# Where the low parts of split weights and of the indexer's doubled keys and queries are subtracted: from GpSimd to VectorE, in the projections of a two-layer hybrid decoder

## The chip, the cores and the metric

The kernel runs on one NeuronCore of one Trainium2 chip. The metric is the device time of one execution, in microseconds (us); lower is better. The engines are named as the profile names them: PE (TensorE; PEld is its weight load), DVE (VectorE), ACT (ScalarE), POOL (GpSimd) and SP (the queue that issues most transfers). Each engine takes its instructions strictly in the order of its own queue.

## The reference, cut to what matters

Two layers work on 1024 prompt tokens and 32 sample tokens (8 sequences of 4). In each layer a normalised activation `h` goes through one combined input projection, whose columns feed four groups of heads; then come attention and recurrences, an output projection, and a gated feed-forward block.

```python
h = rmsnorm(x, lp["norm1_g"]) * (1.0 + sc1) + sh1
p = split_cols(h @ lp["w_in"])
...
sc = jnp.einsum("bqhd,bsd->bqhs", iq, ik).astype(jnp.float32) * IDX_DIM ** -0.5
score = jnp.einsum("bqh,bqhs->bqs", iw.astype(jnp.float32) * IDX_HEADS ** -0.5, jax.nn.relu(sc))
score = jnp.where(k_pos[None, :] <= q_pos[:, None], score, -jnp.inf)
val, idx = lax.top_k(score, topk)
```

The last four lines are the indexer: 8 small heads give each query a score for each key, and the 256 best keys are kept.

## The kernel before, in words

A product of float32 matrices is made from three products of rounded parts: each operand is split into a high part (the value in the matmul's fp32r format) and a low part (value less high part), and high x high, high x low and low x high are summed in PSUM (`dense_c`, line 478, and `dense_n`, line 498). For weights the split is done by `unit` (line 453): a block of 1024 x 256 weights arrives in two halves of 128 x 1024 elements in `wr`; for each half ACT casts it to `wh` (line 461), and POOL subtracts `wh` from `wr` and writes `wl` (line 462). Two blocks of `wh` and `wl` exist at a time, so the cast for a block waits until PE has finished the block two before it.

In a layer the stages follow each other: input projection with the indexer and the top-k selection, attention and recurrences, output projection, feed-forward block. The input projection has twelve such blocks: `idx_q` in `first_units`, then `lru_x` and `lru_gate` (`t_unit`), seven blocks by `nat_unit`, and `gla_q`/`gla_k` and `gla_g` (`t_unit`). After each tile of a projection `background` advances side work: the indexer (`idx_prompt`), its top-k (`topk_prompt`), the samples' index and selection, and the RG-LRU. The output projection and the feed-forward block call `unit` too; at the start of each layer a small block of 128 columns (`misc_aps`) is split as well.

The indexer's keys and queries are doubled in place by `dup` (line 737): each 32-wide vector is laid out as high and low part, ACT casting (line 743) and POOL subtracting (line 744), into tiles of 128 x 512 (`ikd`, `iqd`). The attention code calls the same `dup` for its own tiles (`dup`, 128 x 1024).

The top-k of the prompt runs on DVE and ACT: for each of 31 bits a round compares six rows of scores with a threshold and counts (line 833 on DVE for four of the rows, tiles `tkb` and `tku`; line 830 on ACT for the other two, tile `tks`), and then updates the threshold by a few instructions on 128 x 6 elements (lines 852 to 858, 879 to 885 on DVE). Then six rows are finished with a scan (line 903). The samples' selection does the like with 128 x 1 elements (lines 1001 to 1063). The rotary embedding of a projected tile is two multiplications on DVE and POOL (lines 526, 528, 529) and an addition on DVE (line 530).

The order on each engine is made by a scheduler, which plays the program through a timeline of its own when the kernel is built, and emits the instructions as they come up there. Any change of an instruction's engine therefore moves many others.

```python
def unit(wp, rp, aps, width, n=2, first=None):
    ...
        with soon(HP2):
            act.copy(hi[:, ks, :width], raw[:, :, :width])
            pool.tensor_tensor(lo[:, ks, :width], raw[:, :, :width], hi[:, ks, :width].bitcast(F32), op=sub)
```

Of the kernel before, what the change touches and what calls it, by code (L numbers as in the profile page):

```python
# [10 lines left out]
F32 = mybir.dt.float32  # L11
# [129 lines left out]
def trunk(ctx, tc, io, out, dbg=None, depth=DEPTH, stop=99):  # L141
    nc = tc.nc
    dve, act, pool, pe, sp = nc.vector, nc.scalar, nc.gpsimd, nc.tensor, nc.sync
    mult, add, sub = OP.mult, OP.add, OP.subtract
# [56 lines left out]
    def soon(n):  # L201
        return tc.high_priority(n) if n else nullcontext()
# [230 lines left out]
    def raw_piece(rp, aps, width, i, n, nr):  # L433

        kk = 8 // n
        raw = rp.tile([128, kk, 256], F32, tag="wr", name="wr", bufs=nr)
        if sum(a.shape[1] for _, a in aps) < width:
            pool.memset(raw[:, :, :width], 0.0)
        for c0, a in aps:
            sp.dma_start(raw[:, :, c0:c0 + a.shape[1]],  # L440
                         a[kk * 128 * i:kk * 128 * (i + 1), :].rearrange("(k p) m -> p k m", p=128))
        return raw
# [4 lines left out]
    def weights(name):  # L447

        rp = tc.tile_pool(reuse_waits="tile", name="wr" + name, bufs=2)
        wp = tc.tile_pool(reuse_waits="tile", name="w" + name, bufs=2)  # L450
        return rp, rp.__enter__(), wp, wp.__enter__()

    def unit(wp, rp, aps, width, n=2, first=None):

        hi = wp.tile([128, 8, 256], F32R, tag="wh", name="wh", bufs=2)
        lo = wp.tile([128, 8, 256], F32R, tag="wl", name="wl", bufs=2)
        for i in range(n):
            raw = first[i] if first else raw_piece(rp, aps, width, i, n, 2)
            ks = slice(8 // n * i, 8 // n * (i + 1))
            with soon(HP2):  # L460
                act.copy(hi[:, ks, :width], raw[:, :, :width])  # L461
                pool.tensor_tensor(lo[:, ks, :width], raw[:, :, :width], hi[:, ks, :width].bitcast(F32), op=sub)  # L462
        return hi, lo

    def split2(parts_, c, g, raw):
# [173 lines left out]
    wrpool, wrp, wpool, wp_ = weights("0")  # L639
    mw = unit(wp_, wrp, misc_aps(0), 128)  # L640
    for l in range(depth):
# [25 lines left out]
        def background():  # L667
            advance(side, TK)
            advance(tops, TT)
            if count[0] % ADH == 0:  # L670
                advance(late)
            count[0] += 1
            if count[0] % SELH == 0:
                advance(sel)

        def col(name, c0=0, n=256):
            return w_in[:, OFF[name] + c0:OFF[name] + c0 + n]

        def nat_unit(name):
            w = unit(wp_, wrp, [(0, col(name))], 256)  # L680
            for i in range(9):
                nat_tile(name, w, i)
                background()
# [14 lines left out]
                sp.dma_start(st[name][t0:t0 + n, :], nat[:n, :])  # L698

        def t_unit(specs, aps, width):  # L700
            w = unit(wp_, wrp, aps, width)
            for j, (key, n) in enumerate(specs):
                def done(c, cs, p):
                    with soon(HP1):
                        e = hp.tile([128, CWM], F32, tag="nat", name="te", bufs=3)[:, :CHK[c][1]]
                        act.copy(e, p)
                        sp.dma_start(stt[key][:n, cs], e[:n, :])
                    background()
                dense_t(w, j, h, done, HPD)

        def first_units():

            rope_t.append(const("rope", where=hp).rearrange("p (i w) -> p i w", i=9))
            w = unit(wp_, wrp, [(0, col("idx_q"))], 256)
            mtp = tc.tile_pool(reuse_waits="tile", name="mt", bufs=1)
            mt = mtp.__enter__().tile([128, T], F32, name="mt")
            for c, (c0, cn) in enumerate(CHK):
                act.copy(mt[:, c0:c0 + cn], dense_c(mw, 0, h, c))
                for i in range(3 * c, 3 * c + 3):
                    nat_tile("idx_q", w, i)  # L720
                for i in range(3 * c, 3 * c + 3):
                    t0, n = TOK[i]
                    pm = bank("m")
                    pe.transpose(pm[:n, :128], mt[:, t0:t0 + n], ident)
                    nat = hp.tile([128, CWM], F32, name="nat", bufs=3)[:, :256]
                    raw = hp.tile([128, 256], F32, name="rraw", bufs=2)
                    act.copy(raw[:n, 0:32], pm[:n, 32:64])
                    act.copy(nat[:n, 32:40], pm[:n, 64:72])
                    tmp = hp.tile([128, 256], F32, name="rtm", bufs=2)
                    rope(nat[:n, 0:32], raw[:n, 0:32], i, n, 32, tmp[:n, 0:32], rope_t[0])  # L730
                    sp.dma_start(st["idx_k"][t0:t0 + n, :], nat[:n, 0:32])
                    sp.dma_start(st["idx_w"][t0:t0 + n, :], nat[:n, 32:40])
            sp.dma_start(stt["gla_a"], mt[0:16, :])
            mtp.__exit__(None, None, None)


        def dup(dst, src, nh, d, key):

            dv = dst.rearrange("p (n a b d) -> p n a b d", n=nh, a=2, b=2)
            s = src[:, :, None, :].to_broadcast([128, nh, 2, d])  # L740
            hi = dv[:, :, :, 0, :] if key else dv[:, :, 0, :, :]
            lo = dv[:, :, :, 1, :] if key else dv[:, :, 1, :, :]
            act.copy(hi, s)
            pool.tensor_tensor(lo, s, hi.bitcast(F32), op=sub)

        def stack_t(dst, srcs, idr=None):

# [10 lines left out]
        def idx_prompt():  # L758
            with tc.tile_pool(reuse_waits="tile", name="ix", bufs=2) as ix:
                kn = ix.tile([128, 8, 32], F32, name="ikn", bufs=1)  # L760
# [1 line left out]
                sp.dma_start(wix, st["idx_w"][0:TP, :].rearrange("(i p) d -> p i d", p=128))  # L762
                dve.tensor_scalar(wix, wix, 1.0 / 16.0, None, op0=mult)
                kd = ix.tile([128, 8 * 128], F32R, name="ikd", bufs=1)
                dup(kd, kn, 8, 32, True)
                kst = ix.tile([128, TP], F32R, name="ikst", bufs=1)
                yield
                stack_t(kst, [kd[:, i * 128:i * 128 + 128] for i in range(8)])
# [2 lines left out]
                def prep(i):  # L771
                    qn = ix.tile([128, 8, 32], F32, name="iqn")
                    sp.dma_start(qn, st["idx_q"][i * 128:i * 128 + 128, :].rearrange("p (h d) -> p h d", h=8))
                    qd = ix.tile([128, 8 * 128], F32R, name="iqd", bufs=1)
                    dup(qd, qn, 8, 32, False)
                    Q[i] = ix.tile([128, 8 * 128], F32R, name="iqst")
                    yield
                    stack_t(Q[i][:, :512], [qd[:, j * 128:j * 128 + 128] for j in range(4)])
                    yield
                    stack_t(Q[i][:, 512:], [qd[:, j * 128:j * 128 + 128] for j in range(4, 8)])  # L780
                yield from prep(2)
                for i in range(2, 8):
                    nxt = prep(i + 1) if i < 7 else iter(())
                    n = NB[i]
                    s = sc[:, so[i]:so[i] + n]
# [1261 lines left out]
        n = 0  # L2047
# [52 lines left out]
        wrpool, wrp, wpool, wp_ = weights(f"{l + 1}")  # L2100
# [54 lines left out]
        if True:  # L2155
# [58 lines left out]
            for q in range(11):  # L2214
# [67 lines left out]
                if q % 2 or q == 10:  # L2282
                    n = 4 if q % 2 else 2
# [8 lines left out]
                if pend is not None and q < 10:  # L2292
                    w = down_w(pend[0])
# [68 lines left out]
```

## Time and profile before

| | us |
|---|---|
| median of 3 runs | 3873.0 (3866.61 to 3873.54) |
| the profiled execution, its own time | 3873.57 |
| its span, first to last instruction | 3871.7 |
| mean granted TensorE clock | 0.948 of full speed |

| engine | busy us | share of the span |
|---|---|---|
| PE | 3522.8 | 91% |
| DVE | 2487.2 | 64% |
| ACT | 1502.2 | 39% |
| POOL | 1394.5 | 36% |

Busy is the time in which an engine has an instruction under way, including time in which that instruction is held up. The shares are means over stages with different limits; what bounds one stage is read from that stage alone.

### The profile page before, as it was taken

How to read it: one execution, taken by the hardware profiler on the slowest of the kernel's cores; microseconds unless marked ns; L12 is line 12 of the kernel's file. 1: busy time of each engine (PE TensorE's matmuls, PEld its weight loads, DVE VectorE, ACT ScalarE, POOL GpSimd, SP SyncE). 2: the span in 40 equal slices, each digit the busy share in tenths (PEclk: the TensorE clock that was granted, in tenths of full speed). 3: DMA queues.
4: the chain of work that ended last, by engine and by line, in shares of the span. 5: the costliest groups of instructions: out<-in, count | busy, mean ns of one | idle time of the engine just before them, and what ended most of it. 6: DMA issues, size and time to landing. Idle time of an engine off the chain costs nothing.

```text
span 3871.7 us, 64297 instructions
## 1 busy us (share of the span) xinstructions
PE 3522.8 (91%) x24916; PEld 3150.6 (81%) x24916; DVE 2487.2 (64%) x5662; ACT 1502.2 (39%) x3026; POOL 1394.5 (36%) x1241
## 2 busy tenths in 40 slices
PE   7999868899899999999989988588997999999998
PEld 4887765576689999999979877455766999999997
DVE  5479999677555444445564999985764655555555
ACT  4445554366533112211244547434764322112122
POOL 2344238524233222222334541564343223222231
PEclk7999888989999999999989999788999999999999
DMA  6452335536521332321123222455464011111111
GB/s 228 135 151 89 111 112 184 192 107 203 166 85 50 98 105 87 99 77 34 55 79 92 88 88 71 132 183 195 139 217 152 25 44 51 49 40 49 45 46 56
DMA packets 351404, 407.65 MB, mean 105 GB/s; under 512 B 93711, under 2 KB 299261, under 8 KB 349914
## 3 DMA queue, kind: packets, MB, share of 16 engines
q1 hardware_dynamic: 312186, 265.09, 22.6%
q0 software_dynamic: 38912, 138.43, 10.7%
q8 instruction: 197, 3.23, 0.3%
q14 instruction: 109, 0.89, 0.1%
HBM read 354.32 MB, written 58.04 MB: 107 GB/s over the span
## 4 chain that ended last, share of the span: by engine, by line
PE 65%; DVE 20%; issue 5%; DMA 4%; ACT 3%; POOL 2%; SPq 0%; another core or an unknown queue 0%; DVEq 0%; ACTq 0%; POOLq 0%
PE d L478 31%; PE m L2180 13%; DVE tkb L833 2%; PE d L1369 2%; DVE tku L833 2%; PE d L498 2%; PE e L1399 2%; PE e L1376 1%; PE m L1637 1%; PE d L330 1%; PE g L1796 1%; DVE ny L413 1%; PE m L1689 1%; DVE nat L526 1%; PE m L1696 1%
## 5 line engine op out<-in xcount | busy, mean ns | idle before, releaser
L478 PE MATMUL d<-h,wh 128*128 128x384 f32 (+1 forms) x5856 | 1406.8, 326 | 55.9 <-ACT h L468 18.0
L478 PEld LDWEIGHTS d<-h,wh 128*128 128x128 f32 x5856 | 1031.6, 190 | 72.0 <-ACT h L468 18.5
L478 PE MATMUL d<-h,wl 128*128 128x384 f32 (+1 forms) x2928 | 945.9, 326 | 7.5 <-POOL wl L462 7.5
L478 PEld LDWEIGHTS d<-h,wl 128*128 128x128 f32 x2928 | 557.2, 191 | 11.2 <-POOL wl L462 10.0
L462 POOL TENSOR_TENSOR wl<-wr,wh 128x1024 fp32r<-128x1024 f32 (+1 forms) x172 | 376.9, 2208 | 430.8 <-ACT wh L461 343.6
L498 PE MATMUL d<-wh,h 128*128 128x256 f32 (+1 forms) x2304 | 463.0, 296 | 46.8 <-ACT nat L697 28.5
L498 PEld LDWEIGHTS d<-wh,h 128*128 128x128 f32 (+1 forms) x2304 | 370.8, 191 | 65.7 <-ACT nat L697 32.7
L507 DVE SCALAR_TENSOR_TENSOR xT<-m,mod,xT 128x384 f32<-128x384 f32 (+1 forms) x480 | 273.2, 572 | 230.9 <-PE m L2180 230.4
L2180 PE MATMUL m<-mh,wdh 128*128 128x384 f32 (+1 forms) x1056 | 350.9, 332 | 0.4 <-DVE xT L507 0.4
L2279 POOL TENSOR_TENSOR ml<-z,mh 128x384 fp32r<-128x384 f32 x132 | 132.8, 1025 | 600.2 <-ACT mh L2278 600.2
L2180 PE MATMUL m<-ml,wdh 128*128 128x384 f32 (+1 forms) x1056 | 344.5, 326 | 0.0
L498 PE MATMUL d<-wl,h 128*128 128x256 f32 (+1 forms) x1152 | 338.4, 294 | 5.2 <-POOL wl L462 3.2
L2180 PE MATMUL m<-mh,wdl 128*128 128x384 f32 (+1 forms) x1056 | 342.5, 325 | 0.0
L461 ACT CAST wh<-wr 128x1024 fp32r<-128x1024 f32 (+1 forms) x172 | 158.1, 955 | 200.1 <-PE d L478 169.2
L498 PEld LDWEIGHTS d<-wl,h 128*128 128x128 f32 (+1 forms) x1152 | 220.2, 191 | 12.2 <-issue 6.2
L2250 DVE COPY fs<-G 128x2 f32<-128x2 f32 x44 | 50.8, 1156 | 278.2 <-ACT G L2230 278.2
L2230 ACT COPY G<-d 128x384 f32<-128x384 f32 x132 | 57.4, 442 | 420.3 <-PE d L478 392.4
L2180 PEld LDWEIGHTS m<-mh,wdh 128*128 128x128 f32 x1056 | 200.4, 190 | 9.1 <-issue 6.6
L2180 PEld LDWEIGHTS m<-ml,wdh 128*128 128x128 f32 x1056 | 200.6, 190 | 1.4 <-issue 0.9
L2180 PEld LDWEIGHTS m<-mh,wdl 128*128 128x128 f32 x1056 | 200.3, 190 | 0.0
L2170 POOL TENSOR_TENSOR wdl<-wr,wdh 128x1024 fp32r<-128x1024 f32 x44 | 104.9, 2416 | 264.0 <-ACT wdh L2169 264.0
L1369 PE MATMUL d<-c_ident,kv 128*128 128x128 f32 x1024 | 165.1, 295 | 16.3 <-ACT KT L210 7.5
(554 smaller groups left out, 6664.7 us busy)
## 6 DMA issues: line engine op xcount, KB each, us to landing
adaw<-in_w_ada_dram SPq DMA_DIRECT2D x80, 512.0 KB
wr<-in_w_in_dram SPq DMA_DIRECT2D x48, 512.0 KB
wr<-in_ffn_w_gate_dram SPq DMA_DIRECT2D x44, 512.0 KB
wr<-in_ffn_w_up_dram SPq DMA_DIRECT2D x44, 512.0 KB
wr<-in_ffn_w_down_dram SPq DMA_DIRECT2D x44, 512.0 KB
xd<-xT SPq DMA_DIRECT2D x16, 528.0 KB
adaw<-in_w_ada_dram SPq DMA_DIRECT2D x8, 1024.0 KB
wr<-in_w_out_dram SPq DMA_DIRECT2D x32, 256.0 KB
```

Of the source, the lines that this page charges most:

```text
L461: act.copy(hi[:, ks, :width], raw[:, :, :width])
L462: pool.tensor_tensor(lo[:, ks, :width], raw[:, :, :width], hi[:, ks, :width].bitcast(F32), op=sub)
L478: pe.matmul(pd, lhsT=w[a][:, k, j * 128:j * 128 + 128], rhs=h[b][c][:, k, :], start=(q == 0), stop=(q == 23))
L498: pe.matmul(pd[:n, :256], lhsT=h[b][c][:, k, t0:t0 + n], rhs=w[a][:, k, :], start=(q == 0), stop=(q == 23))
L507: dve.scalar_tensor_tensor(x[:, m, t0:t0 + n], p[:, :n], mod[:, gate + m, 0:1], x[:, m, t0:t0 + n], op0=mult, op1=add)
L833: dve.tensor_scalar(scratch[:, :n], src[:, s], thr[:, j:j + 1], None, op0=OP.is_ge, op1=add, accum_out=cnt[:, j:j + 1])
L1369: pe.transpose(pm[:, z_ * 128:z_ * 128 + 128], kg[:, j, f * 128:f * 128 + 128], ident)
L1399: pe.matmul(po[32 * j:32 * j + 32, :256], lhsT=wT[:, g, 32 * j:32 * j + 32], rhs=vg[:, j, :], start=(g == 0), stop=(g == 3))
L2170: pool.tensor_tensor(lo[:, z_, :], raw, hi[:, z_, :].bitcast(F32), op=sub)
L2180: pe.matmul(pd, lhsT=a, rhs=b, start=(n == 0), stop=(n == len(ops) - 1))
L2230: act.copy(Gp[:, 2 + CHK[c][0]:2 + CHK[c][0] + n], p[:, :n])
L2279: pool.tensor_tensor(ml[:, cs], z[:, cs], mh[:, cs].bitcast(F32), op=sub)
```

## The change

`unit` and `dup` get a parameter `eng`, by default POOL. The input projection's callers pass DVE: the twelve blocks of each layer (24 subtractions of 128 x 1024 elements a layer), and the indexer's seven tiles (128 x 512). The small block at a layer's start, the output projection, the feed-forward block and the attention's `dup` keep POOL. The arithmetic is the same.

```diff
-    def unit(wp, rp, aps, width, n=2, first=None):
+    def unit(wp, rp, aps, width, n=2, first=None, eng=pool):
...
                 act.copy(hi[:, ks, :width], raw[:, :, :width])
-                pool.tensor_tensor(lo[:, ks, :width], raw[:, :, :width], hi[:, ks, :width].bitcast(F32), op=sub)
+                eng.tensor_tensor(lo[:, ks, :width], raw[:, :, :width], hi[:, ks, :width].bitcast(F32), op=sub)
...
         def nat_unit(name):
-            w = unit(wp_, wrp, [(0, col(name))], 256)
+            w = unit(wp_, wrp, [(0, col(name))], 256, eng=dve)
...
         def t_unit(specs, aps, width):
-            w = unit(wp_, wrp, aps, width)
+            w = unit(wp_, wrp, aps, width, eng=dve)
...
         def first_units():
...
-            w = unit(wp_, wrp, [(0, col("idx_q"))], 256)
+            w = unit(wp_, wrp, [(0, col("idx_q"))], 256, eng=dve)
...
-        def dup(dst, src, nh, d, key):
+        def dup(dst, src, nh, d, key, eng=pool):
...
             act.copy(hi, s)
-            pool.tensor_tensor(lo, s, hi.bitcast(F32), op=sub)
+            eng.tensor_tensor(lo, s, hi.bitcast(F32), op=sub)
...
-                dup(kd, kn, 8, 32, True)
+                dup(kd, kn, 8, 32, True, dve)
...
-                    dup(qd, qn, 8, 32, False)
+                    dup(qd, qn, 8, 32, False, dve)
```

Two places show how the order moves. The first is on DVE, in the first layer's top-k, at the start of the 27th round of counting (`tku`: the compare-and-count of line 833; `tdf`, `tth`, `tcd`, `tnc`: the threshold's update; `wl`: the low part of the weights). Before:

```order
L884 TENSOR_TENSOR tdf<-cnt,tneed 128x6
L1040 TENSOR_SCALAR sdl<-spc 128x1
L885 SCALAR_TENSOR_TENSOR tth<-tdf,tth 128x6
L1041 SCALAR_TENSOR_TENSOR scand<-sdl,scand 128x1
L879 TENSOR_SCALAR tcd<-tth 128x6
L881 TENSOR_SCALAR tnc<-tth 128x6
L1037 TENSOR_SCALAR snc<-scand,scap 128x1
L833 TENSOR_SCALAR tku,cnt<-mk,tcd 128x384
L833 TENSOR_SCALAR tku,cnt<-mk,tcd 128x640
L833 TENSOR_SCALAR tku,cnt<-mk,tcd 128x768
```

With the change:

```order
L885 SCALAR_TENSOR_TENSOR tth<-tdf,tth 128x6
L879 TENSOR_SCALAR tcd<-tth 128x6
L881 TENSOR_SCALAR tnc<-tth 128x6
L1150 TENSOR_SCALAR lth_4995<-lth_4995,spt 128x1056
L833 TENSOR_SCALAR tku,cnt<-mk,tcd 128x384
L462 TENSOR_TENSOR wl<-wr,wh 128x1024
L833 TENSOR_SCALAR tku,cnt<-mk,tcd 128x640
L462 TENSOR_TENSOR wl<-wr,wh 128x1024
L1001 STREAM_TRANSPOSE srep<-scnt 128x32
L833 TENSOR_SCALAR tku,cnt<-mk,tcd 128x768
```

The two subtractions of the last block (`gla_g`) now stand inside the round, between its counts; before, they stood on POOL.

The second place is on ACT, at the casts that these two subtractions wait for (`tks`: ACT's counts, two a round; `nat`: the copy of a projected tile out of PSUM; `wh`: the cast). Before:

```order
L830 ACTIVATE tks,cnt<-mk,tnc 128x512
L1017 ACTIVATE selb,scnt<-ss,snc,sng 128x544
L697 COPY nat<-d 128x256
L830 ACTIVATE tks,cnt<-mk,tnc 128x896
L1146 ACTIVATE lth_4995<-m,hb 128x288
L697 COPY nat<-d 32x256
L461 CAST wh<-wr 128x1024
L1017 ACTIVATE selb,scnt<-ss,snc,sng 128x544
L461 CAST wh<-wr 128x1024
```

With the change:

```order
L1017 ACTIVATE selb,scnt<-ss,snc,sng 128x544
L830 ACTIVATE tks,cnt<-mk,tnc 128x512
L830 ACTIVATE tks,cnt<-mk,tnc 128x896
L1146 ACTIVATE lth_4995<-m,hb 128x288
L697 COPY nat<-d 32x256
L461 CAST wh<-wr 128x1024 x2
L1017 ACTIVATE selb,scnt<-ss,snc,sng 128x544
L830 ACTIVATE tks,cnt<-mk,tnc 128x512
```

Before, these casts stood behind 56 of ACT's counts, which is 28 rounds; with the change they stand behind 52, which is 26 rounds. The copy of the last `gla_v` tile stays just ahead of them.

## Rows read from the trace of the kernel before

**Rows 1.** The page's first line.

```profile
span 3871.7 us, 64297 instructions
```

**Rows 2.** Stretches: length, busy PE, PEld, DVE, ACT, POOL, clock, DMA share, GB/s.

```profile
130.00:195.00 65.00, 62.77 (x517) 56.38 (x515) 18.31 (x30) 27.63 (x56) 14.40 (x11) 0.97 0.54 159
390.00:455.00 65.00, 53.48 (x374) 49.52 (x372) 64.17 (x216) 40.34 (x78) 15.72 (x17) 0.89 0.35 110
2325.00:2390.00 65.00, 54.35 (x386) 50.35 (x386) 63.71 (x198) 46.01 (x89) 18.62 (x7) 0.97 0.29 90
```

**Rows 3.** Line 462, whole span: ns min/median/max, first and last start in us.

```profile
L462 POOL TENSOR_TENSOR wl<-wr,wh x172: 1261/2393/2984, 57.6 to 3759.2; 128x1024 fp32r<-128x1024 f32 x136, 128x512 fp32r<-128x512 f32 x36
```

**Rows 4.** Timeline of POOL: start, us, instruction, count.

```profile
299.07 4.72 POOL L462 TENSOR_TENSOR wl<-wr,wh 128x1024 fp32r<-128x1024 f32 x2
...
338.16 4.72 POOL L462 TENSOR_TENSOR wl<-wr,wh 128x1024 fp32r<-128x1024 f32 x2 [0.28 <-issue]
```

**Rows 5.** Timeline of DVE, first layer: a count and an update, then ten instructions.

```profile
301.61 1.28 DVE L833 TENSOR_SCALAR_CACHE_REDUCE tkb<-mk,cand 128x1024 bf16<-128x1024 bf16 x1
304.07 0.17 DVE L858 SCALAR_TENSOR_TENSOR cand<-dlt,cand 128x6 int32<-128x6 int32 x1
...
338.23 2.34 DVE L858 SCALAR_TENSOR_TENSOR cand<-dlt,cand 128x6 int32<-128x6 int32 x1
340.61 2.29 DVE L852 SCALAR_TENSOR_TENSOR tnc<-cand,tcap 128x6 f32<-128x6 f32 x1
...
380.54 2.69 DVE L872 SCALAR_TENSOR_TENSOR mk<-mk,cand,tku 128x640 uint16<-128x640 bf16 x1
383.15 2.61 DVE L526 TENSOR_TENSOR nat<-rraw,c_rope 32x256 f32<-32x256 f32 x1
...
416.63 2.36 DVE L879 TENSOR_SCALAR tcd<-tth 128x6 f32<-128x6 f32 x1
419.24 2.29 DVE L881 TENSOR_SCALAR tnc<-tth 128x6 f32<-128x6 f32 x1
...
459.56 2.07 DVE L1041 SCALAR_TENSOR_TENSOR scand<-sdl,scand 128x1 int32<-128x1 int32 x1
461.79 2.15 DVE L884 TENSOR_TENSOR tdf<-cnt,tneed 128x6 f32<-128x6 f32 x1
...
493.94 2.98 DVE L1150 TENSOR_SCALAR lth<-lth,spt 128x1056 f32<-128x1056 f32 x1
496.83 2.35 DVE L879 TENSOR_SCALAR tcd<-tth 128x6 f32<-128x6 f32 x1
```

**Rows 6.** Timeline of DVE, second layer: the first and the last of eight.

```profile
2149.03 5.25 DVE L530 TENSOR_TENSOR nat<-nat,rtm 32x256 f32<-32x256 f32 x1 [0.77 <-POOL rtm L529]
...
2386.74 2.17 DVE L884 TENSOR_TENSOR tdf<-cnt,tneed 128x6 f32<-128x6 f32 x1
```

**Rows 7.** Timeline of DVE: a wide operation on two SBUF tensors, and its successor.

```profile
440.41 1.25 DVE L1163 TENSOR_TENSOR lth<-lth,la 128x1056 f32<-128x1056 f32 x1
441.58 0.87 DVE L833 TENSOR_SCALAR_CACHE_REDUCE tku<-mk,tcd 128x640 uint16<-128x640 uint16 x1
```

**Rows 8.** Waits from 260 to 520 us: us in total, times, longest us.

```profile
PE d L498 <- ACT nat L697: 17.0, 12, 4.0
```

**Rows 9.** Timeline of ACT: the second of the first layer's last casts.

```profile
494.88 1.03 ACT L461 CAST wh<-wr 128x1024 fp32r<-128x1024 f32 x1
```

**Rows 10.** Timeline of DVE: first count of the round where the subtractions now stand.

```profile
484.43 0.60 DVE L833 TENSOR_SCALAR_CACHE_REDUCE tku<-mk,tcd 128x384 uint16<-128x384 uint16 x1
```

**Rows 11.** Timeline of DVE: the last scan of the top-k, each layer.

```profile
559.24 2.28 DVE L903 TENSOR_TENSOR_SCAN sc<-tku,one 128x1024 f32<-128x1024 bf16 x1
...
2460.52 2.27 DVE L903 TENSOR_TENSOR_SCAN sc<-tku,one 128x1024 f32<-128x1024 bf16 x1
```

**Rows 12.** Chain that ended last: start, us, what; the output projection's first loads.

```profile
1056.35 6.96 DMA mixr<-mix
...
2958.64 7.70 DMA mixr<-mix
```

## The prediction
> **What bounds the kernel now.** I read the page first, for the span [rows 1], and then the table of stretches, because the change touches only the two projection stages and a mean over the whole span says nothing about them. Early in the stage PE is the full engine: 62.8 of 65 us from 130 us on, while DVE has 18.3 [rows 2]. From the top-k on it is DVE: 64.2 and 63.7 of 65 us in stretches of the two layers, with PE at 53.5 and 54.4 [rows 2]. There the stage ends when DVE has worked off its queue; PE and ACT follow it. What comes behind takes the same time in both layers: from the start of the last scan of the top-k to the first load of the output projection are 497.1 us (559.24 to 1056.35) and 498.1 us (2460.52 to 2958.64) [rows 11, 12], although the scheduler gave the two attention stages different orders. So I count what DVE gains or loses in the top-k one to one.
>
> Next I read the timelines of POOL and DVE side by side. A subtraction of 1024 elements takes POOL 2.39 us [rows 3], and they come in pairs, as at 338.16 for 4.72 us [rows 4]. Just then DVE's updates, which take 0.17 us when undisturbed, take 2.34 and 2.29 us [rows 5]. The same is seen at the pairs that follow: ten instructions in the first layer are stretched so [rows 5]. A count of line 833 is not: the one at 301.61 runs inside POOL's pair of 299.07 and takes its usual 1.28 us [rows 4, 5]. So "busy" DVE is, for some microseconds per pair, a DVE that is held up by POOL's subtraction.
>
> The Trainium skill, "SBUF — State Buffer", section "Who interferes with whom", says that a VectorE instruction with two SBUF inputs, or in a two-port mode, and a GpSimd instruction that reads SBUF exclude each other, the first to start holding the ports for its whole length. The trace agrees, down to the accumulating counts that are spared.
>
> **The change part by part.** *Removed: the hold-ups.* The ten stretched rows of the first layer sum to 24.1 us. Their own work is seven small ones at 0.17 us, 1.2 us, and three wider ones (256, 640 and 1056 elements), which I put at 0.4, 0.8 and 1.25 us in proportion to the 1.25 us of a 1056-element operation [rows 7]: 3.65 us in all, so 20.5 us are hold-up. In the second layer eight instructions are stretched, the first and the last shown [rows 6]; they sum to 25.9 us, of which four of 256 elements (1.6 us) and four small ones (0.7 us) are work: 23.6 us. Together **44 us** on the bounding engine. Bounds: 39.4 us if each wider instruction were worth 1.25 us, 48 us if they were worth nothing.
>
> *Added: the subtractions on DVE.* The trace shows none there. The nearest row is a subtraction-like operation on two SBUF tensors of 1056 elements: 1.25 us long, its successor starting 1.17 us after it [rows 7]. I take 1.2 us. Where DVE is the bound stand, in the new order, the pair cast near 299 us and five later ones in the first layer and seven pairs in the second: 26 x 1.2 = **31 us**. The bounds: 28 us if one took a tenth less, 62 us if it took POOL's 2.39 us [rows 3]. I stay by the DVE row, since it is the same kind of operation on the same engine; the upper end would give 3893 us, and is one more reason for a wide upper side.
>
> *Friction.* The new subtraction has two SBUF inputs, so POOL's remaining operations can hold it up. In the stretch from 390 us POOL is busy 15.7 us [rows 2], less a pair of some 4.7 us [rows 4]: a sixth of the time. 26 x 1/6 x half a microsecond is **2 us**; from below 0.
>
> *The other 22 of the 48, and the indexer's 14.* They stand where DVE has room (18.3 of 65 us) [rows 2]; I put them at nothing, and what hides them is PE's queue of projections. If that cover failed at the norm that opens a layer, four subtractions in each layer would cost 2 x 4 x 1.2 = 10 us, but POOL's subtraction holds up DVE's norm there too, so part comes back. For PE the low part comes a little sooner per half (1.2 against 2.39 us of making), or later where DVE's queue is full; the double buffer hides either. SP's and POOL's transfers are neither added nor taken away; POOL's gathers lose a neighbour ahead of them.
>
> *Sum.* 44 - 31 - 2 = 11 us less. Against the profiled execution's own 3873.57 us, which is 0.6 us above the median of the runs, that is **3862 us**.
>
> **The rivals.** *1. DVE waits for the cast (slower).* On POOL a subtraction that stood waiting for ACT's cast cost nothing. On DVE everything behind it waits: the counts, the updates, and through them ACT's counts and PE's banks. In the old trace the second cast of `gla_g` ends at 494.88 + 1.03 = 495.9 us [rows 9], and the round in which the new order puts its subtractions starts at 484.43 us [rows 10]; DVE would reach the second subtraction about 1.5 us later. That is 10 us of standing still; with one such block in each layer 20 us, and 3862 + 20 = **3882 us**. What speaks against it: the order of ACT shows these casts behind 52 counts in place of 56, two rounds earlier, and two rounds are at least 2 x (0.60 + 0.87 + 0.87 + 1.28) = 7 us of counts alone [rows 5, 7, 10]; and PE, which must first finish the `gla_v` tile, has time in hand, since it waited 17.0 us for ACT's copies in that stretch [rows 8]. It decides from the point where the cast is more than about 5.5 us late per layer: then the 11 us are gone.
>
> *2. The stage passes to PE and ACT (no change).* PE is busy 53.5 of 65 us at a clock of 0.89 [rows 2]. If the last projection blocks become the end of the stage, part of the gain stays unused; with 3 of the 11 us left it is about **3870 us**. Against it: after the last block DVE alone still finishes the six rows, up to 559 us [rows 11].
>
> *3. The hold-up turns round (no change).* A subtraction on DVE may in its turn hold up POOL's rotary multiplication, and DVE's addition of line 530 then waits for that, each time up to 1.2 us. If a quarter of the 26 meet one, 8 us come back: **3870 us**. The Trainium skill, "Perfetto Trace Analysis", section "Optimizing Scalar/DVE Operations", warns in this sense that offloading between VectorE and GpSimd might not help, because they share an SBUF read port; by that rule the time would be this rival's. The trace bears it out only for POOL holding up DVE. Against it: POOL is idle for three quarters of the stretch from 390 us [rows 2], and the holding time is half of today's.
>
> *4. The stretched rows are no hold-up (slower).* If these instructions waited for something else that stays, only the addition is left: 3873.6 + 31 = **3905 us**. Against it: eighteen stretched rows, all inside a pair of POOL.
>
> **How the numbers follow.** I give the forecast 0.53, rival 1 0.18, rival 2 0.18, rival 3 0.07, rival 4 0.04. A measurement of this kernel can tell about 0.2%, 7.7 us, from no change: faster is below 3865.3, slower above 3880.7. Part of the forecast's own range (3852 to 3869: lock and price at their nearer bounds) lies inside that band, and a part of rivals 2 and 3 below it: faster 0.50, same 0.28, slower 0.22. Downwards the range takes in that PE's 17.0 us of waiting for copies [rows 8] is released as well and shortens the early part of the window: 3862 - 17 = 3845. Upwards it takes in rival 1 with some more: 3886. Rival 4 and a worse rival 1 stay outside.
>
> **What would show it.** Right: in the new trace the ten rows' counterparts (lines 852 to 885, 1041) take 0.17 us throughout, line 462 on DVE takes 1.2 to 1.3 us, and the last scans of the top-k start some 5 us earlier against each layer's start. Rival 1 shows as idle time of DVE ahead of line 462, released by ACT's cast. Rival 2 shows as DVE idle in the top-k, waiting for ACT's `tks` or for PE; rival 3 as waits of line 530 for POOL's `rtm`. The prediction is wrong if DVE's subtraction takes 2 us or more, or if the small updates stay long.

## The result and the profile after

The changed kernel takes 3818.6 us (median of 4 runs, 3813.52 to 3821.69), the kernel before 3869.81 us beside it (the three runs shown ahead and one more, 3861.11 to 3873.54). The ratio is 0.9868, with a 95% interval of 0.9855 to 0.9881: **51 us or 1.3% faster**. The prediction was 3862 us, 11 us faster, with a range of 3845 to 3886. The sign was right; the result lies below the range, and the gain is more than four times the one foretold.

The page of the changed kernel begins as follows. Its profiled execution took 3821.09 us, at a mean granted clock of 0.956 (before 0.948).

```profile
span 3819.3 us, 64298 instructions
...
PE 3494.2 (91%) x24916; PEld 3125.7 (82%) x24916; DVE 2452.0 (64%) x5724; ACT 1500.7 (39%) x3026; POOL 1271.7 (33%) x1179
```

DVE has 62 instructions more and is busy 35 us less (2487.2 before). Line 462, over the whole span (instruction, tile, count, ns min/median/max, first and last start):

```profile
L462 POOL TENSOR_TENSOR wl<-wr,wh x124: 1261/2394/2714, 57.8 to 3706.2; 128x1024 fp32r<-128x1024 f32 x88, 128x512 fp32r<-128x512 f32 x36
L462 DVE TENSOR_TENSOR wl<-wr,wh x48: 1149/1219/1521, 73.6 to 2328.9; 128x1024 fp32r<-128x1024 f32 x48
```

48 subtractions went from 2.39 us on POOL [rows 3] to 1.22 us on DVE; the prediction took 1.2. Here is the round of the top-k in which the last block's subtractions now stand, in DVE's timeline (start, us, instruction):

```profile
466.08 0.16 DVE L884 TENSOR_TENSOR tdf<-cnt,tneed 128x6 f32<-128x6 f32 x1
...
466.33 0.15 DVE L885 SCALAR_TENSOR_TENSOR tth<-tdf,tth 128x6 f32<-128x6 f32 x1
466.52 0.17 DVE L879 TENSOR_SCALAR tcd<-tth 128x6 f32<-128x6 f32 x1
466.60 0.17 DVE L881 TENSOR_SCALAR tnc<-tth 128x6 f32<-128x6 f32 x1
466.67 0.77 DVE L1150 TENSOR_SCALAR lth<-lth,spt 128x1056 f32<-128x1056 f32 x1
...
467.88 1.22 DVE L462 TENSOR_TENSOR wl<-wr,wh 128x1024 fp32r<-128x1024 f32 x1
469.02 0.87 DVE L833 TENSOR_SCALAR_CACHE_REDUCE tku<-mk,tcd 128x640 uint16<-128x640 uint16 x1
469.81 1.22 DVE L462 TENSOR_TENSOR wl<-wr,wh 128x1024 fp32r<-128x1024 f32 x1
```

Lines 884, 879, 881 and 1150, which took 2.15 to 2.98 us in [rows 5], take 0.16 to 0.77 us here. Not all short instructions are free: POOL's multiplications of the RG-LRU still stretch a few of them to 2.3 and 2.4 us (see e9). Three stretches, with the columns of [rows 2]; the second and third lie where those of [rows 2] lay, counted from the first update of line 858 in each layer:

```profile
130.00:195.00 65.00, 62.41 (x515) 57.18 (x516) 24.65 (x40) 28.31 (x58) 0.77 (x2) 0.97 0.54 161
381.69:446.69 65.00, 56.35 (x415) 52.67 (x415) 64.55 (x205) 42.57 (x83) 14.89 (x13) 0.95 0.38 118
2284.77:2349.77 65.00, 56.95 (x375) 54.27 (x375) 63.74 (x197) 50.77 (x97) 7.42 (x3) 0.95 0.21 68
```

In the top-k DVE is as full as before; PE is busier beside it (56.4 and 57.0 us against 53.5 and 54.4).

**Where the 52 us went.** I set four marks in each layer: the first update of the top-k (line 858), the last copy of the input projection out of PSUM (line 706 on ACT), the last scan of the top-k (line 903), the first load of the output projection. The first two, in the kernel before (timelines of DVE and of ACT):

```profile
290.65 0.17 DVE L858 SCALAR_TENSOR_TENSOR cand<-dlt,cand 128x6 int32<-128x6 int32 x1
...
2200.68 0.17 DVE L858 SCALAR_TENSOR_TENSOR cand<-dlt,cand 128x6 int32<-128x6 int32 x1
```

```profile
553.07 0.40 ACT L706 COPY te<-d 128x288 f32<-128x288 f32 x1 [1.34 <-PE d L478]
...
2442.84 0.76 ACT L706 COPY te<-d 128x384 f32<-128x384 f32 x2
```

The changed kernel, timeline of DVE, then of ACT, then the loads in the chain that ended last:

```profile
282.34 0.17 DVE L858 SCALAR_TENSOR_TENSOR cand<-dlt,cand 128x6 int32<-128x6 int32 x1
...
533.55 2.27 DVE L903 TENSOR_TENSOR_SCAN sc<-tku,one 128x1024 f32<-128x1024 bf16 x1
...
2160.45 0.17 DVE L858 SCALAR_TENSOR_TENSOR cand<-dlt,cand 128x6 int32<-128x6 int32 x1
...
2424.61 2.63 DVE L903 TENSOR_TENSOR_SCAN sc<-tku,one 128x1024 f32<-128x1024 bf16 x1
```

```profile
525.78 0.38 ACT L706 COPY te<-d 128x288 f32<-128x288 f32 x1
...
2381.18 0.76 ACT L706 COPY te<-d 128x384 f32<-128x384 f32 x2
```

```profile
1020.92 7.57 DMA mixr<-mix
...
2904.53 6.17 DMA mixr<-mix
```

Step by step, with [rows 11, 12] for the other marks of before:

| stage | before | after | difference |
|---|---|---|---|
| start to first update, layer 1 | 290.7 | 282.3 | -8.3 |
| first update to last projection copy | 262.4 | 243.4 | **-19.0** |
| last copy to output projection | 503.3 | 495.1 | -8.1 |
| to first update, layer 2 | 1144.3 | 1139.5 | -4.8 |
| first update to last projection copy | 242.2 | 220.7 | **-21.4** |
| last copy to output projection | 515.8 | 523.4 | +7.6 |
| output projection to end | 913.1 | 914.8 | +1.7 |

So 40 of the 52 us lie between the first update and the last projection copy, 13 ahead of the first update, and the rest cancels. Adding up in the old trace by how much each DVE instruction delays the next one beyond its own usual length while POOL's line 462 runs gives some 21 and 20 us in those two stretches, about what they lost. Ahead of the first updates, back to the start of each input projection, the same sum gives some 43 us more, so some 84 us in all. The subtractions that now stand in the two stretches (12 and 10, busy 15.0 and 12.4 us) go with last copies that come sooner, not later. The last scan came 6.2 and 17.7 us after the last copy before, and comes 7.8 and 43.4 us after it now. In the second layer recurrence work (lines 1885 to 1890) stands on DVE in between. In these tails PE is busy 1.2 of 7.4 and 8.3 of 42.7 us, at the lower of its two clock levels (columns of [rows 2]), so it is not PE's work that covers them; what does is not shown:

```profile
526.16:533.55 7.39, 1.23 (x3) 1.07 (x4) 6.60 (x19) 1.02 (x4) 0.00 (x0) 0.50 0.55 155
2381.90:2424.61 42.71, 8.31 (x17) 5.10 (x18) 41.69 (x102) 18.01 (x33) 14.20 (x23) 0.51 0.45 114
```

PE's stretch in the same two windows, before and after (columns of [rows 2]):

```profile
290.65:553.47 262.82, 225.65 (x1549) 203.17 (x1547) 253.09 (x711) 148.39 (x300) 87.90 (x78) 0.94 0.28 89
2200.68:2442.80 242.12, 206.06 (x1379) 183.63 (x1377) 234.41 (x657) 140.15 (x281) 83.16 (x79) 0.95 0.25 80
```

```profile
282.34:526.16 243.82, 216.83 (x1539) 194.69 (x1538) 238.99 (x716) 146.54 (x298) 67.10 (x69) 0.98 0.31 96
2160.45:2381.20 220.75, 195.85 (x1353) 176.01 (x1351) 214.27 (x662) 140.91 (x284) 55.06 (x66) 0.98 0.27 84
```

PE's idle time falls from 37.2 to 27.0 and from 36.1 to 24.9 us. It is also 8.8 and 10.2 us less busy; 10 and 26 matmuls fewer stand in the windows, but one takes 141 and 145 ns in place of 146 and 149 (busy time by count), and that makes 7 and 6 us of it. The granted clock, a mean of its two levels of 2.4 and 1.2 GHz, is 0.98 in place of 0.94 and 0.95. A way by which a stall of DVE can reach PE is ACT, which counts for the same rounds and copies PE's tiles. From 260 to 520 us PE's waits for ACT's copies fell from 17.0 us [rows 8] to

```profile
PE d L498 <- ACT nat L697: 8.2, 6, 2.6
```

### The profile page after: what moved, and what is told of

Its sections match the earlier page's. It is cut to its first block, busy times and chain, and to the rows that moved or that the text cites. A ratio compares the mean times of both kernels' runs of the same rounds, so it can differ in the third digit from the quotient of the medians.

```text
span 3819.3 us, 64298 instructions
## 1 busy us (share of the span) xinstructions
PE 3494.2 (91%) x24916; PEld 3125.7 (82%) x24916; DVE 2452.0 (64%) x5724; ACT 1500.7 (39%) x3026; POOL 1271.7 (33%) x1179
## 4 chain that ended last, share of the span: by engine, by line
PE 68%; DVE 19%; DMA 4%; issue 4%; ACT 3%; POOL 1%; SPq 1%; another core or an unknown queue 0%; DVEq 0%; ACTq 0%; POOLq 0%
PE d L478 31%; PE m L2180 13%; PE d L498 4%; PE d L1369 3%; DVE tku L833 3%; DVE tkb L833 2%; PE e L1399 2%; PE e L1376 1%; PE m L1637 1%; PE d L330 1%; PE m L1696 1%; DVE ny L413 1%; PE g L1796 1%; PE m L753 1%; PE m L1689 1%
## 5 line engine op out<-in xcount | busy, mean ns | idle before, releaser
L498 PE MATMUL d<-wh,h 128*128 128x256 f32 (+1 forms) x2304 | 450.3, 291 | 34.3 <-ACT nat L697 16.1
L498 PEld LDWEIGHTS d<-wh,h 128*128 128x128 f32 (+1 forms) x2304 | 360.3, 186 | 56.3 <-ACT nat L697 19.6
L462 POOL TENSOR_TENSOR wl<-wr,wh 128x1024 fp32r<-128x1024 f32 (+1 forms) x124 | 259.8, 2112 | 310.3 <-ACT wh L461 244.3
```

Source lines behind the costliest of these rows:

```text
L462: eng.tensor_tensor(lo[:, ks, :width], raw[:, :, :width], hi[:, ks, :width].bitcast(F32), op=sub)
L498: pe.matmul(pd[:n, :256], lhsT=h[b][c][:, k, t0:t0 + n], rhs=w[a][:, k, :], start=(q == 0), stop=(q == 23))
```

## The experiments

The runs were made on several chips, on which the kernel before took between 3843 and 3873 us; so I compare ratios to the kernel before, run beside each, and turn them into microseconds with its median there. The theories are **H** (POOL's reading subtraction holds DVE up, and this was counted too small), **Q** (POOL's queue was the trouble, not what it reads), and **O** (the scheduler's new order gave most of the gain by chance).

**The change in parts.** e1: weights alone; e2: the indexer's doublings alone; e3: `idx_q`, `lru_x`, `lru_gate` and the doublings; e4: the `nat` and `gla` blocks alone.

```diff
-                dup(kd, kn, 8, 32, True, dve)
+                dup(kd, kn, 8, 32, True)
...
-                    dup(qd, qn, 8, 32, False, dve)
+                    dup(qd, qn, 8, 32, False)
```

That is e1; e2 has the two lines as changed and the three calls of `unit` without `eng=dve`. e4 has e1's two lines, POOL for `idx_q`, and in `t_unit` the following; e3 is the opposite, with POOL in `nat_unit` too.

```diff
-            w = unit(wp_, wrp, aps, width, eng=dve)
+            w = unit(wp_, wrp, aps, width, eng=dve if specs[0][0].startswith("gla") else pool)
```

> Only the 48 weight subtractions on DVE; the indexer's 14 stay on POOL. Theory H (the gain is hold-up taken off DVE, counted too small): those 14 hold DVE up for 2.4 us in all in the old trace, so nearly all of the gain stays: 3817 to 3823 us. Theory Q (the gain in the early part comes from POOL's queue being free for the indexer and the rotary multiplications): the 14 x 1.3 us on POOL stay, and the weights' 24 early ones go: also nearly all, 3820 to 3828. Theory O (the new order made by the scheduler, not the hold-ups, gave the 40 us beyond the forecast): a change this small throws the order again, and the time may fall anywhere between 3815 and 3865.

> Only the indexer's 14 doublings on DVE; all weight subtractions on POOL. H: 2.4 us of hold-up go, 14 x 0.69 us are added where DVE has room: 3867 to 3873, no change. Q: POOL's queue keeps the weights' 2.4 us: 3864 to 3870. O: as likely 3830 as 3870, since the order is thrown again.

> Indexer's doublings and the blocks idx_q, lru_x and lru_gate on DVE; the nat and gla blocks on POOL as before. In the changed kernel the stretch up to the first top-k round was 8.3 us shorter in the first layer and 3.9 us in the second. H and Q: about that much, 12 us, is all that this half gives: 3855 to 3862. O: no relation to the place of the subtractions; 3820 to 3870.

> The nat and gla blocks on DVE; idx_q, lru_x, lru_gate and the doublings on POOL as before. H: the rest of the gain, 51 - 12 = 39 us: 3827 to 3835; with e3 the two gains add up to some 51 us. O: the two gains do not add up to 51 by more than 10 us.

| run | ratio | 95% interval | against before |
|---|---|---|---|
| e1 weights | 0.9862 | 0.9846 to 0.9879 | -53 us |
| e2 doublings | 1.0018 | 1.0009 to 1.0028 | +7 us |
| e3 early | 0.9987 | 0.9978 to 0.9997 | -5 us |
| e4 late | 0.9898 | 0.988 to 0.9917 | -39 us |

The weights make the whole gain; the doublings cost a little. Early and late add up to 44 us, near the 51 to 53 of the whole, as H said and O did not. In e4 the first layer's stretch from first update to last copy is 243.9 us long, as in the changed kernel (243.4), under an order with thousands of rows elsewhere; in e2 and e3 it is 262.7 and 261.9, as before. The early part gives 5 us, not the 12 expected.

**The hold-up put back, and POOL kept busy without reading.** Both add to the changed kernel, behind each of the 48 subtractions, work of POOL on the raw weights, which nobody needs any more.

```diff
                 eng.tensor_tensor(lo[:, ks, :width], raw[:, :, :width], hi[:, ks, :width].bitcast(F32), op=sub)
+                (eng is dve) and pool.tensor_tensor(raw, raw, hi[:, ks, :].bitcast(F32), op=sub)
```

This is e5 (the added call stands on line 462 too, so that the line numbers stay). e6 adds in its place:

```diff
+                (eng is dve) and (pool.memset(raw, 0.0), pool.memset(raw, 0.0))
```

> The changed kernel, and after each of the 48 subtractions on DVE the same subtraction once more on POOL, its result thrown away (written over the raw weights). It brings POOL's hold on DVE back without taking anything from DVE. Theory H (POOL's reading holds DVE up, and each microsecond of it stands on the path of the whole stage, whichever engine looks full): the ratio to the kernel before goes from 0.987 to above 1.000, by what the 48 subtractions cost on DVE: 3 to 62 us above before. With the sums of the prediction (hold-up 44 us against the changed kernel): 0.998. Theory Q (POOL's queue, not the port): the same rise, but then the next run rises too. Theory O (the order): the time stays within 15 us of the changed kernel, 0.985 to 0.991.

> The changed kernel, and after each of the 48 subtractions on DVE two fills of the same 128x1024 raw weights on POOL, about 2 us of POOL's time that reads nothing. H: DVE's small updates stay at 0.17 us and the time stays at the changed kernel's, 0.985 to 0.990 of before. Q: as the run before, 0.995 or more. O: anything from 0.983 to 0.995.

> The kernel before once more, for its trace on this chip: the marks of the stages are compared with those of the other runs. All theories: the ratio is 1, and the eight pairs of POOL in the top-k of each layer hold DVE up by 20 us or so.

e5 came to **1.0028** (1.0011 to 1.0045), 62 us above the changed kernel's ratio and 11 us above the kernel before. e6 came to **0.9909** (0.9887 to 0.9932), 16 us above the changed kernel, with an interval that nearly touches it. POOL's timeline in e5, then DVE's:

```profile
418.57 2.53 POOL L462 TENSOR_TENSOR wr<-wr,wh 128x1024 f32<-128x1024 f32 x1 [2.42 <-DVE wl L462]
422.61 2.38 POOL L462 TENSOR_TENSOR wr<-wr,wh 128x1024 f32<-128x1024 f32 x1 [1.51 <-DVE sp_a L1103]
```

```profile
417.29 1.21 DVE L462 TENSOR_TENSOR wl<-wr,wh 128x1024 fp32r<-128x1024 f32 x1
418.76 2.35 DVE L1102 TENSOR_TENSOR sp_a<-sp_a,sp_z 128x2 f32<-128x2 f32 x1
...
423.12 1.88 DVE L1102 TENSOR_TENSOR sp_a<-sp_a,sp_z 128x2 f32<-128x2 f32 x1
```

An addition of two elements takes 2.35 us, to the end of POOL's repeated subtraction. First update to last copy is back at 259.8 and 242.1 us, at a granted clock of 0.94 and 0.95; in e0, the kernel before on that chip, it is 262.9 and 242.2. With the fills of e6 it is 247.0 and 225.1, near the changed kernel's 243.4 and 220.7. POOL is busy 86.2 and 72.5 us there, against 67.1 and 55.4 in the changed kernel and 93.0 and 84.2 in e5: the fills add some two thirds of what the repeated subtractions add, and if POOL's time were the cause, some 40 of e5's 62 us would have come. So H holds, and Q falls, though e6's 0.9909 lies just above the range that H gave it (0.985 to 0.990). Most of e6's 16 us lie behind the attention, where its code is that of the changed kernel (924.5 us from the first load of the second output projection to the end, against 914.8); why is left open.

That PE waited for POOL's slower making of the low part is another way to explain the gain. It does not fit: e5 makes the low part on DVE as the changed kernel does, and is as slow as before.

**Work on DVE doubled, and taken away.** e7 makes each of the 48 subtractions twice on DVE. e8 makes none: POOL fills the low parts with zeros.

```diff
                 eng.tensor_tensor(lo[:, ks, :width], raw[:, :, :width], hi[:, ks, :width].bitcast(F32), op=sub)
+                (eng is dve) and eng.tensor_tensor(lo[:, ks, :width], raw[:, :, :width], hi[:, ks, :width].bitcast(F32), op=sub)
```

```diff
-                eng.tensor_tensor(lo[:, ks, :width], raw[:, :, :width], hi[:, ks, :width].bitcast(F32), op=sub)
+                pool.memset(lo[:, ks, :width].bitcast(F32), 0.0) if eng is dve else eng.tensor_tensor(lo[:, ks, :width], raw[:, :, :width], hi[:, ks, :width].bitcast(F32), op=sub)
```

> The changed kernel with each of the 48 subtractions on DVE made twice. It prices the term 'added': 31 us (26 of 48 on the path) by the prediction: 0.995 of before. If all 48 are on the path: 48 x 1.2 = 58 us, 1.002. If DVE has room for them after all (the top-k's end does not set the end of the stage): 0 to 10 us, 0.987 to 0.990, and then the prediction's error is that term.

> The changed kernel with the 48 weight subtractions of the input projections left out on every engine: POOL fills the low parts with zeros in their place (a write that reads nothing), so the low parts of these weights are missing from the output. Neither hold-up nor work on DVE: before less this run is what the hold-ups cost, this run less the changed kernel is what the subtractions cost on DVE. By the terms of the prediction (44 and 31 us): 0.9886, slower than the changed kernel, which cannot be; so at least one term is wrong. If the term 'hold-ups' was short (84 us of stretched instructions in the whole of both stages, 0.7 us of time for each, as the run with POOL's repeated subtraction gave) and the subtractions cost little: 0.980 to 0.985. If the 48 subtractions cost 60 us, as the doubled ones did, and the hold-ups 110: 0.970 to 0.974.

e7 came to **1.0023** (1.0012 to 1.0034): 60 us for 48 more subtractions, 1.25 us each. e8 came to **0.9842** (0.9815 to 0.987). So the hold-ups cost 61 us (1 less 0.9842 of 3869 us; 50 to 72 by the interval), which agrees with the 62 of e5, and the first 48 subtractions cost 10 us (0.9868 less 0.9842; the intervals allow from nothing to 25), which agrees with the 11 by which e5 stands above before. The first updates, the last copies, the first layer's last scan and the output projections' first loads in e8 (DVE, ACT, DVE, chain that ended last):

```profile
280.96 0.30 DVE L858 SCALAR_TENSOR_TENSOR cand<-dlt,cand 128x6 int32<-128x6 int32 x1
...
2160.05 0.15 DVE L858 SCALAR_TENSOR_TENSOR cand<-dlt,cand 128x6 int32<-128x6 int32 x1
```

```profile
524.53 0.38 ACT L706 COPY te<-d 128x288 f32<-128x288 f32 x1
...
2396.84 0.38 ACT L706 COPY te<-d 128x288 f32<-128x288 f32 x1
```

```profile
524.99 2.28 DVE L903 TENSOR_TENSOR_SCAN sc<-tku,one 128x1024 f32<-128x1024 bf16 x1
```

```profile
1024.65 7.42 DMA mixr<-mix
...
2898.74 7.34 DMA mixr<-mix
```

The first layer's first update, last copy and last scan in e7 (DVE, ACT, DVE):

```profile
288.80 0.17 DVE L858 SCALAR_TENSOR_TENSOR cand<-dlt,cand 128x6 int32<-128x6 int32 x1
```

```profile
528.25 0.76 ACT L706 COPY te<-d 128x384 f32<-128x384 f32 x2
```

```profile
576.93 2.55 DVE L903 TENSOR_TENSOR_SCAN sc<-tku,one 128x1024 f32<-128x1024 bf16 x1
```

Counted from the first update, the first layer's last copy stands at 243.6 us with no subtraction, 243.4 with twelve (the changed kernel) and 239.4 with twenty-four; the last scan at 244.0, 251.2 and 288.1. So there work on DVE does not delay the projections; it makes the top-k's tail behind them longer, from 0.5 to 7.8 to 48.7 us.

The second layer does not bear this out in the same way. Its last copy stands at 236.8 us with no subtraction, 220.7 with ten and 211.7 with twenty (e7, from 2206.68 to 2418.37): with neither hold-up nor subtraction the stretch is only 5 us shorter than before (242.2), with DVE's subtractions 21 us. The new order moves work to either side of this mark, so the 21.4 us of the table are not shown to be hold-up alone, and a shorter stretch is not in itself a gain. Nor did the granted clock rise with the hold-ups gone: e8 has 0.97 in the first layer's stretch and 0.94 in the second's. Over a wider stretch, from the first update to the output projection, the two layers together take 1523.7 us before, 1482.7 with the change and 1482.4 in e8: by these profiles 41 us come there from taking the hold-ups away, and the subtractions cost nothing in sum. The rest of the span falls from 2348.0 to 2336.6 and, in e8, 2329.2.

**Both terms, by part.** The late blocks without their subtractions and with doubled ones (e12, e13, on e4), the early ones likewise (e14, e15, on e3), by the lines of e7 and e8.

> As e4 (0.990: nat and gla blocks on DVE, all else on POOL), but with those 36 subtractions left out (POOL fills the low parts with zeros, which therefore are missing from the output). By the prediction's terms: hold-ups 44 us, subtractions 31 us: 0.9886 and 0.008 below e4, which do not agree with each other. If the whole of what was missed lies in the top-k: hold-ups 60 us, 0.984 to 0.985. If it lies in the early part: 0.988 to 0.989, and the subtractions cost next to nothing there.

> As e4 (0.990), with its 36 subtractions made twice on DVE. If extra work on DVE costs its full length in the top-k: 36 x 1.2 = 43 us, 1.001. If it costs what the first ones cost (about 0.2 us each): 0.992. If the price grows because slack is used up: in between or above, 0.996 to 1.003.

> As e3 (0.9987: idx_q, lru_x, lru_gate and the doublings on DVE, the rest on POOL), but with those 12 weight subtractions left out, so that their low parts are missing. The prediction put both the early hold-ups and the early subtractions at nothing: 0.998 to 1.001. If early hold-ups count as the late ones do (the first three blocks of each layer hold DVE up for some 8 to 12 us a layer): 0.993 to 0.996.

> As e3 (0.9987), with its 12 weight subtractions made twice on DVE. By the prediction (DVE has room there): 0.998 to 1.000. If the early part is as dear as the late: 12 x 1.2 = 14 us, 1.002. If the doubled subtractions also make PE wait for the low part, more than that: 1.003 to 1.006.

| blocks | left out | on DVE once | on DVE twice | so: hold-ups | first set | second set |
|---|---|---|---|---|---|---|
| late, 36 subtractions | e12 0.983 (0.9813 to 0.9846) | e4 0.9898 | e13 1.0005 (0.9995 to 1.0015) | 65 us | 26 us | 41 us |
| early, 12 | e14 0.9947 (0.9931 to 0.9964) | e3 0.9987 | e15 0.9981 (0.9972 to 0.9991) | 20 us | 15 us | none |

In the early part hold-ups and subtractions nearly cancel. In the late part the hold-ups are dear and the first 36 subtractions cost 0.7 us each; the second 36 cost 1.1. In the old trace DVE is held up for some 64 us by the late blocks' subtractions on POOL and some 20 us by the early ones' (the sum of above, split by block), so by parts a microsecond of hold-up costs about a microsecond; by e8, 61 of 84 us, it costs 0.7. The parts do not add up to the whole (65 and 20 against 61; 26 and 15 against 10): each kernel has an order of its own and e3, e14 and e15 carry the doublings too, so a part is known to some 10 us only.

**More of the same.** On e1: e9 moves the RG-LRU's six wide multiplications of each layer (lines 1182, 1186, 1187) to DVE, e10 the rotary multiplications (528, 529), e11 the differential attention's doublings.

```diff
-                    pool.tensor_tensor(a2, a2, g, op=mult)
+                    dve.tensor_tensor(a2, a2, g, op=mult)
...
-        pool.tensor_tensor(u[:, :, 0, :], s[:, :, 1, :], nsin[:, None, :].to_broadcast([n, nh, half]), op=mult)
+        dve.tensor_tensor(u[:, :, 0, :], s[:, :, 1, :], nsin[:, None, :].to_broadcast([n, nh, half]), op=mult)
...
-                dup(dd, src.rearrange("p i (m d) -> p (i m) d", m=2), 16, 32, iskey)
+                dup(dd, src.rearrange("p i (m d) -> p (i m) d", m=2), 16, 32, iskey, dve)
```

> The weights' subtractions on DVE, the indexer's doublings on POOL (as in e1, 0.986), and in addition the six two-input multiplications of 128x1056 elements in each layer's RG-LRU (lines 1182, 1186, 1187) moved from POOL to DVE. In the changed kernel they hold DVE up for some 9 us in each top-k. H (what reads two inputs on POOL during the top-k costs what it holds up): 18 us less, 12 x 1.25 = 15 us more on DVE: 0.984 to 0.987. If a subtraction on DVE costs much less than its length: 0.981 to 0.984. O: 0.982 to 0.992.

> As e1 (0.986), and in addition the rotary multiplications of lines 528 and 529 on DVE. They are short (0.65 us each on POOL) and DVE waits for them before line 530. H: the waits of line 530 (5 to 11 us a layer) go, 72 x 0.2 us of work a layer are added: 0.984 to 0.988. If DVE's own work is what counts in the top-k: 0.988 to 0.992.

> As e1 (0.986), and in addition the doublings of the differential attention's tiles (line 744, 128x1024) on DVE. In the attention stage DVE is busy 355 of 487 us and PE sets the pace. H: little to gain, since DVE has room for its held-up time there: 0.984 to 0.988. If hold-ups count in every stage: below 0.983.

e9: 0.9892 (0.9866 to 0.9918), 12 us above e1, with intervals that overlap. e10: 0.998 (0.9967 to 0.9993), 46 us above e1. e11: 0.9851 (0.9821 to 0.9882), not to be told from e1. e9 and e10 came out above what was expected of them. In e10 (line 528 over the whole span, then line 529, the same form):

```profile
L528 DVE TENSOR_TENSOR rtm<-rraw,c_rope x108: 155/284/1011, 85.6 to 2283.1; 128x128 f32<-128x128 f32 x80, 128x16 f32<-128x16 f32 x16, 32x128 f32<-32x128 f32 x10, 32x16 f32<-32x16 f32 x2
...
L529 DVE TENSOR_TENSOR rtm<-rraw,c_rope x108: 156/284/819, 85.8 to 2283.3; 128x128 f32<-128x128 f32 x80, 128x16 f32<-128x16 f32 x16, 32x128 f32<-32x128 f32 x10, 32x16 f32<-32x16 f32 x2
```

The 216, of 0.28 us in the median, are 59 us of work, and 46 us came of it: after the change DVE has little room left. The six multiplications of e9 remove their hold-up (9 us a layer) for 12 x 1.25 = 15 us of work; by a price of a microsecond for each that is a gain of 3 us, and none came. So the price found for the weights is not a rule for every instruction that POOL holds DVE up with. No version here that computes the whole is clearly faster than the changed kernel.

## Why the prediction was wrong, point by point

- *The stretched rows are a hold-up by POOL's subtraction.* Right, and shown: e5 brings them back, e8 takes them away with only fills on POOL in their place. Rival 4 falls.
- *"Together 44 us on the bounding engine."* **This is the step that failed**: a term mis-sized. The hold-ups cost 61 to 62 us (e8, e5). The rows that were counted were read rightly, and pricing them one to one was, if anything, too much: the hold-ups cost 0.7 (e8) to 1.0 us (e12, e14) for each microsecond of stretch. But the sum began at the pair of 338 us in the first layer and of 2149 us in the second. The pairs ahead of these hold DVE up for some 35 of the 84 us, and they were put at nothing; that DVE has room there is said of the subtractions alone. They count: the early blocks' hold-ups alone cost 20 us (e14).
- *"I count what DVE gains or loses in the top-k one to one"*, and so *31 us* for the subtractions. By the whole kernel **this step failed too**. The duration was right (1.219 us, the longest 1.521, so that little friction was seen), its price in time was not: 10 to 11 us for all 48 (e8, with nothing to 25 by the intervals; e5). In the first layer the projections' last copy comes at nearly the same time with 0, 12 or 24 subtractions, so DVE's queue is not what ends them; that was rival 2's point, and it helped in place of hurting. The runs by part put the price higher (26 us for the late 36, 15 for the early 12), so its size stays open. The two terms of the whole together: 61 less 10 is 51, the measured gain. The sign was no luck: hold-ups cost more than the subtractions in every pair of runs (61 against 10, 65 against 26, 20 against 15).
- *What comes behind takes the same time whatever its order.* Measured from the last scan it does not: 497.1 us became 487.4 and 498.1 became 479.9. From the last projection copy on the two layers changed by -8.1 and +7.6 us, which cancel. The last scan was a poor mark: in the second layer recurrence work was put ahead of it.
- *The other 22 subtractions and the 14 doublings cost nothing.* The 14 cost 7 us (e2), the early 12 cost 15 (e3 less e14), paid for by the early hold-ups.
- *Rival 1* (DVE waits for the cast): not in the top-k, where DVE's waits of the changed kernel name no cast; ahead of it DVE waited 7.4 us in the first layer, where it had room.
- *Rival 3* (the hold-up turns round): no gain was foretold by it, and 1.3% came. The Trainium skill, "Perfetto Trace Analysis", section "Optimizing Scalar/DVE Operations", warns that moving work between VectorE and GpSimd might not help because they share a read port. Here the hold-up, which the page puts down to that port, is the reason why it did help: POOL needs 2.39 us for what DVE does in 1.22, and holds DVE up meanwhile. The other way round little was seen: in the top-k of the changed kernel no wait of DVE names POOL's `rtm`.

That a microsecond of hold-up costs more than one of added work, at first, is shown in size only: 0.7 us by e8 (61 of 84), against 0.2 for the first 48 subtractions (10 of 59) and 1.0 for the next 48 (e7). My reading is that the order is made with the added work in view and without the hold-up: a planned subtraction is put where DVE has work to spare, while a stall strikes whatever update stands there, with ACT's counts and PE's banks waiting for it. This was not tried, and a kernel with a fixed order would be needed to show it.

## What to carry to other kernels

When one engine stretches another one's short instructions, add up the stretch over the whole stage, also where the stretched engine looks half idle: here 84 us, while the full stretch alone gave 44, and 61 came back. Before counting added work one to one, look for the mark at which the next stage really starts; and try a mark in every layer and in a run without the work, since a new order can move work across it. Such room is used up once: the first 48 subtractions cost 10 us, the next 48 cost 60.

## What was not expected of the hardware

POOL's fills hold DVE up too, but other instructions of it. In e6 (POOL, then DVE):

```profile
2342.32 3.88 POOL L462 MEMSET wr<- 128x1024 f32 x4 [13.21 <-DVE wl L462]
```

```profile
2342.46 1.22 DVE L462 TENSOR_TENSOR wl<-wr,wh 128x1024 fp32r<-128x1024 f32 x1
2343.60 1.28 DVE L1131 SCALAR_TENSOR_TENSOR lxa<-lxp,V,lxa 128x1024 f32<-128x1024 f32 x1
2344.79 0.16 DVE L884 TENSOR_TENSOR tdf<-cnt,tneed 128x6 f32<-128x6 f32 x1
...
2345.39 0.84 DVE L879 TENSOR_SCALAR tcd<-tth 128x6 f32<-128x6 f32 x1
2345.46 0.77 DVE L881 TENSOR_SCALAR tnc<-tth 128x6 f32<-128x6 f32 x1
```

While POOL fills, DVE's operations on two tensors run at their usual 0.16 and 1.22 us; the operations on one tensor (0.17 us otherwise) take 0.84 and 0.77 us, to the end of the fill at 2346.20. During POOL's subtraction it was the two-tensor form that was held up as well [rows 5]. The Trainium skill, "SBUF — State Buffer", section "Who interferes with whom", says as much: two SBUF inputs collide with a GpSimd instruction that reads, not with one that only writes, and a two-port mode collides with either. The trace agrees, and so e6 and e8 are not quite free of hold-ups.
